# Eight gate projections in the paired stage, sample tiles of two heads in one, and a normalisation on ScalarE

## Chip, cores and metric

The kernel runs on one core of one Trainium2 chip. The metric is the device time of one execution in microseconds (us); the kernel before takes 1000.45 us in the median of 3 runs (999.62 to 1001.2). Lower is better.

## What is computed

One layer of a streaming encoder, all in float32, on 1024 prompt tokens and 64 sample tokens (T = 1088 together), with D = 1024:

```python
h = rms_norm(x, norm_w) @ w_in                     # 6144 columns
sb_q, sb_k, sb_v, sb_z, cb_q, cb_k, cb_v, cb_z, g_sb, g_cb = split(h)   # 8 heads x 64; gates 1024 columns each
# branch sb, "stick breaking": s < t only
z = q . k / 8
w[t,s] = sigmoid(z[t,s]) * prod_{s<j<t} (1 - sigmoid(z[t,j]));   o_sb = w @ v
# branch cb: softmax over a band of 8 chunks of 64 to the left, with a learned bias
p = softmax(q . k / 8 + bias[clip(q_pos - k_pos)]);   o_cb = p @ v
y = x + (sigmoid(g_sb) * ((o_sb * silu(z_sb)) @ w_proj_sb) + sigmoid(g_cb) * ((o_cb * silu(z_cb)) @ w_proj_cb)) @ w_out
```

The 64 sample tokens attend to a cache of 512 tokens and to themselves (576 keys). New keys and values are outputs too.

## The kernel before

A float32 product is made of three matmuls on a high and a low part of each operand (high x high, high x low, low x high), so every weight tile is split: ScalarE copies the high part (`W.hi`, L115), GpSimd subtracts it for the low part (`W.lo`, L122). Engines run their instructions in the order of the program; all DMAs are issued by SP in program order, besides some of the output.

The stages, in order of the program:

1. Natural projections (L464): q and k of cb and both v, tokens on the rows.
2. The paired stage (L615 to L655). A list `pairs` names blocks of 256 columns of `w_in`, two tiles of 128. Each is computed transposed by seven products instead of eight (Winograd's form of Strassen's scheme, halves of the columns, of D and of the tokens); a product is 2 chunks of 256 and 288 tokens x 12 matmuls (L634). There are 8 pairs: k and q of sb, and the gates z of both branches (kind "silu"). `emit` (L565) also knows a kind "sig", which nothing uses yet: sigmoid on ScalarE, then a store to DRAM (L575).
3. Fill. A list `units` of 16 tiles of 128 columns: eight of g_sb, stored as sigmoid, eight of g_cb, stored plain. `run_fill` (L766) is a generator that issues one matmul a step: a unit is 3 chunks of 384, 384 and 320 tokens x 8 x 3 = 72 matmuls (L773), each chunk evacuated by ScalarE (`ev_act`, L748) and stored. Weights of a later unit are loaded and split on the way (L780 to L785). Behind the units the same generator goes on with the projection of sb's output (`proj_sb`, L855, matmuls of L873). Two units run alone before the attention (L1154 to L1159).
4. The attention (L1169 to L1202). `seq` lists steps: branch, then pair of heads p (4), then tile t (the sample tile t = 8 first, then eight tiles of 128 prompt rows), then head hd. Step i does `qk(i)`, some fill, a weighted sum `av` if one is due, `tr(i-3)`, `mid(i)`, and the rest of its fill.
   - `qk`: scores by two matmuls a half (high and low part of q, L1024, L1025). In sb two sigmoids on ScalarE (L1027, L1028). In cb VectorE adds the bias and takes the row minimum of the negated scores (L1030, one custom instruction a half), and ScalarE takes the exponential with its sum (L1034).
   - `mid`: in sb a scan and a multiply on VectorE (L1044, L1045). In cb a reciprocal (L1047) and a multiply by it (L1048), both VectorE.
   - `tr`: transposes by TensorE (L1076), copied out by ScalarE (L1085, L1081) or VectorE (L1087), in turns set by the counter `flip`.
   - `av`: matmuls with v (L1115), a multiply by z on VectorE (L1118), a store.
   
   `rows(t)` is 64 for the sample tile, so it uses 64 of 128 rows, once per head. The amount of fill of a step is planned: `n_sb` and `n_cb` matmuls in all for each branch (L1161, L1162), shared out in proportion to the number of keys of the step (plus 150 in cb). When cb begins, 12 more are added at each step with t = 8 of its first pair of heads (L1185). The last unit is held back until sb's last output has been stored (L982, L1191).
   Buffers: 3 PSUM tiles for scores (a tile of over 512 keys takes two), 4 for `be`, 3 for `kp`, 4 for the transposed weights.
   `prefetch` (L1123) issues the loads of the next q, k, v and biases at fixed steps. At the start of cb, the biases of its first two heads are loaded (L1177) into memory that sb's tiles give up.
5. The rest of `proj_sb`, the projection of cb (L917), the output product (L1409) and the stores.

Of the kernel before, what the change touches and what calls it, by code (L numbers as in the profile page):

```python
# [17 lines left out]
KT = 8  # L18
# [14 lines left out]
def hybrid_step_kernel(ctx: ExitStack, tc: tile.TileContext, x_prompt, x_sample, c_sbk, c_sbv, c_cbk, c_cbv,  # L33
# [114 lines left out]
    for p in (0, 2):  # L148
        pairs += [("silu", 1536 + 128 * p, d_z["sb"][p:p + 2]), ("silu", 3584 + 128 * p, d_z["cb"][p:p + 2])]
    units = [("ev_act", 4096 + 128 * j, (AF.Sigmoid, d_g["sb"][j])) for j in range(KT)]  # L150
    units += [("ev_act", 5120 + 128 * j, (AF.Copy, d_g["cb"][j])) for j in range(KT)]

# [522 lines left out]
    G.memset(imp[:, 0:896], 0.0)  # L675
    V.tensor_copy(imp[:, 896:1024], ident)

    deferred = []
# [19 lines left out]
    def place_q(dst, src, o0, o1):  # L698

        for hd in range(2):  # L700
            for dup in range(2):
                rdma(dst[dup * 64:dup * 64 + 64, 2 * hd:2 * hd + 2, :o1 - o0], src[hd * 64:hd * 64 + 64, :, o0:o1])

    SQ, KS, VP, BI, st, wT, zts = {}, {}, {}, {}, {}, {}, {}

    def alloc_q(key, ci):
        if ci == 3:
            SQ[key, 3] = am.tile([128, 4, 64], F32R, name="sqs", bufs=1)
# [269 lines left out]
    def fill(n):  # L978
        n += owed[0]
        owed[0] = 0  # L980
        while n > 0:
# [9 lines left out]
    seq = [(b, p, t, hd) for b in ("sb", "cb") for p in range(NPAIR) for t in [8] + list(range(8))  # L991
           for hd in range(2)]

# [8 lines left out]
    def qk(i):  # L1002
        b, p, t, hd = seq[i]
        key = (b, p)
        r = rows(t)
        k0, n = band(b, t)
# [6 lines left out]
        if b == "sb":  # L1013
            kp = ax.tile([128, NP + 2], F32, name="kp", bufs=3)
            G.memset(kp[:r, n:n + 1], 0.0)
        else:
            kp = am.tile([128, 4], F32, name="sm", bufs=6)
            bt = BI[2 * p + hd]
            off = 0 if t == 8 else 640 - n
        for j, (x, y) in enumerate(hs):  # L1020
            z = psZ.tile([128, 512], F32, name="z")
            o = k0 * 128
            m = y - x
            TE.matmul(z[:r, :m], s[:, 2 * hd, q0:q0 + r], ks[:, hd, o + x:o + y], start=True, stop=False)  # L1024
            TE.matmul(z[:r, :m], s[:, 2 * hd + 1, q0:q0 + r], ks[:, hd, o + x:o + y], start=False, stop=True)  # L1025
            if b == "sb":
# [10 lines left out]
    def mid(i):  # L1037
        b, p, t, hd = seq[i]
        r = rows(t)
        k0, n = band(b, t)  # L1040
        be, kp = st[i]
        if b == "sb":
            im = imp[0:64, 960 - n:960] if t == 8 else imp[:, NP - n:NP]
            V.tensor_tensor_scan(kp[:r, n - 1::-1], kp[:r, n - 1::-1], im[:, ::-1], 0.0, op0=OP.mult, op1=OP.add)  # L1044
            V.tensor_tensor(out=be[:r, :n], in0=be[:r, :n], in1=kp[:r, 1:n + 1], op=OP.mult)  # L1045
        else:
            V.reciprocal(kp[:r, 3:4], kp[:r, 2:3])  # L1047
            V.tensor_scalar(be[:r, :n], be[:r, :n], kp[:r, 3:4], None, op0=OP.mult)  # L1048

# [5 lines left out]
    def tr(i):  # L1055
        b, p, t, hd = seq[i]
        r = rows(t)
        k0, n = band(b, t)
# [37 lines left out]
    def av(b, p, j):  # L1096
# [13 lines left out]
        for si, (kb, c0, c1) in enumerate(steps):  # L1110
# [3 lines left out]
            for hd in range(2):  # L1114
                TE.matmul(o[hd * 64:hd * 64 + 64, c0:c1], vv[:kr, kb, hd * 64:hd * 64 + 64],  # L1115
                          wT[b, p, j, hd, s // 4][:kr, s % 4, c0:c1], start=si == 0, stop=si == len(steps) - 1)
        os = zts.pop((b, p, j))
# [28 lines left out]
    def load_bias(h):  # L1146
# [4 lines left out]
        G.memset(bt[64:128, 0:64], BIG)  # L1151
        BI[h] = bt

    load_k("sb", 0, 1)  # L1154
# [5 lines left out]
    FP = 180  # L1160
    n_sb = 72 * 7  # L1161
    n_cb = 72 * (len(units) - 9) + FP  # L1162
    wt = {"sb": lambda n: n, "cb": lambda n: n + 150}
# [5 lines left out]
    for i in range(len(seq) + LAG + 1):  # L1169
# [25 lines left out]
        if 0 <= i - LAG < len(seq):  # L1195
            tr(i - LAG)
            b, p, t, hd = seq[i - LAG]
            if hd == 1 and (t % 2 == 1 or t == 8):
                avq.append((b, p, t // 2 if t < 8 else 4))
# [295 lines left out]
```

## Time and profile before

The profiled execution of the kernel before:

| | |
|---|---|
| median of 3 runs | 1000.45 us |
| span of the profiled execution | 1000.1 us |
| instructions | 20177 |
| granted TensorE clock, mean | 0.998 |
| TensorE matmul busy | 977.8 us |
| VectorE busy | 657.0 us |
| ScalarE busy | 472.9 us |
| GpSimd busy | 324.9 us |
| moved by DMA | 169.83 MB |

Rows of the profile name engines: PE is TensorE (PEld its weight loads), DVE VectorE, ACT ScalarE, POOL GpSimd, SP SyncE, which issues the DMAs (SPq its queue). A group's row gives line, engine, operation, the tile written <- the tiles read, shapes and count, then busy us and mean ns of one, then the idle time of the engine just before these instructions and what ended it. A row of the timeline begins with its start and its length in us. L12 is line 12 of the kernel before; behind the change, lines are moved by 4 to 18.

Matmuls are pipelined, so a busy PE is not PE at its peak, and the times of two neighbours overlap.

### The profile page before, as it was taken

The page shows a single profiled execution, that of the slowest core. Times are in us where ns is not written, and L with a number is a line of the kernel's source. Part 1 is how long each engine was busy: PE and PEld are TensorE (multiplying, and loading weights), DVE is VectorE, ACT ScalarE, POOL GpSimd, SP SyncE. Part 2 cuts the span into 40 slices and gives each one's busy share as a digit, 9 for nine tenths or more (in the row PEclk, how much of TensorE's full clock was granted, in tenths as well). Part 3 has the DMA queues.
Part 4 walks back from the last instruction along what each step waited for, and adds up shares of the span by engine and source line. Part 5 has one row for each costly group of instructions (what it writes and reads, how often), then busy time and mean ns, then how long its engine had stood idle before and what let it go on. Part 6 is the DMA issues. An engine that isn't in the chain of part 4 may idle for free.

```text
span 1000.1 us, 20177 instructions
## 1 busy us (share of the span) xinstructions
PE 977.8 (98%) x7512; PEld 930.8 (93%) x7512; DVE 657.0 (66%) x1233; ACT 472.9 (47%) x1075; POOL 324.9 (32%) x338
## 2 busy tenths in 40 slices
PE   5999999999999999999999999999999899999998
PEld 5999999999999999988898888898989798999998
DVE  5456674895455454099898878565766766499735
ACT  5534443444344433277676656454445434365320
POOL 3276663215445543211111101110202200386552
PEclk9999999999999999999999999999999999999999
DMA  7726577424656332786566544765656854773642
GB/s 237 224 92 221 189 249 256 150 91 150 198 155 192 102 97 85 188 228 187 146 166 159 160 114 117 206 200 152 193 150 186 253 168 147 242 224 101 196 136 89
DMA packets 180865, 169.83 MB, mean 170 GB/s; under 512 B 34912, under 2 KB 167136, under 8 KB 180640
## 3 DMA queue, kind: packets, MB, share of 16 engines
q1 hardware_dynamic: 172048, 160.23, 54.2%
q10 hardware_dynamic: 8720, 8.33, 2.6%
q8 instruction: 59, 0.97, 0.4%
q14 instruction: 38, 0.31, 0.1%
HBM read 109.78 MB, written 58.72 MB: 168 GB/s over the span
## 4 chain that ended last, share of the span: by engine, by line
PE 92%; DMA 2%; DVE 2%; ACT 1%; SPq 1%; issue 1%; POOL 1%; DVEq 0%; ACTq 0%
PE acc L464 19%; PE acc L773 18%; PE b L634 17%; PE b L1409 8%; PE o L1115 7%; PE pt L1076 6%; PE b L917 5%; PE z L1025 3%; PE z L1024 3%; PE acc L873 3%; PE pk L349 1%; DMA wrawx<-in_w_in_dram 1%; DMA gt<-d_gsb 1%; DVE be L1045 1%; PE pt L277 1%
## 5 line engine op out<-in xcount | busy, mean ns | idle before, releaser
L122 POOL TENSOR_TENSOR wlo<-wraw,whi 128x1024 fp32r<-128x1024 f32 x30 | 74.2, 2473 | 243.9 <-ACT whi L115 209.2
L773 PE MATMUL acc<-xm,whi 128*128 128x384 f32 (+1 forms) x384 | 128.5, 335 | 0.0
L1044 DVE TENSOR_TENSOR_SCAN kp<-kp,imp 64x576 f32<-64x576 f32 (+8 forms) x72 | 102.8, 1427 | 21.3 <-ACT kp L1027 21.1
L1034 ACT ACTIVATE be<-be,sm 128x640 f32<-128x640 f32 (+5 forms) x72 | 50.8, 705 | 97.1 <-DVE sm L1030 97.1
L1076 PE MATMUL pt<-ident,be 128*128 128x128 f32 (+2 forms) x608 | 90.1, 272 | 6.4 <-DVE wT L1087 3.4
L1085 ACT ACTIVATE wT<-pt 128x512 f32<-128x512 f32 (+3 forms) x130 | 63.6, 502 | 55.1 <-PE pt L1076 55.1
L1076 PEld LDWEIGHTS pt<-ident,be 128*128 128x128 f32 (+2 forms) x608 | 68.5, 140 | 18.4 <-issue 6.4
L464 PE MATMUL acc<-whi,xa 128*128 128x256 f32 x256 | 74.2, 292 | 0.0
L773 PEld LDWEIGHTS acc<-xm,whi 128*128 128x128 f32 x384 | 72.5, 189 | 1.1
L464 PE MATMUL acc<-wlox,xm 128*128 128x256 f32 x256 | 70.8, 278 | 0.0
L464 PE MATMUL acc<-whi,xm 128*128 128x256 f32 x256 | 70.8, 278 | 0.0
L464 PE MATMUL acc<-wlo,xa 128*128 128x256 f32 x256 | 70.7, 278 | 0.0
L464 PE MATMUL acc<-whix,xb 128*128 128x256 f32 x256 | 70.7, 278 | 0.0
L464 PE MATMUL acc<-whix,xm 128*128 128x256 f32 x256 | 70.6, 278 | 0.0
L1115 PE MATMUL o<-wT,vp 128*64 128x256 f32 (+1 forms) x608 | 66.7, 359 | 0.0
L1045 DVE TENSOR_TENSOR be<-be,kp 64x576 f32<-64x576 f32 (+8 forms) x72 | 60.3, 837 | 9.6
L1027 ACT ACTIVATE kp<-z 128x384 f32<-128x384 f32 (+6 forms) x112 | 54.3, 485 | 24.4 <-PE z L1025 22.9
L773 PE MATMUL acc<-xa,wlo 128*128 128x384 f32 (+1 forms) x192 | 65.4, 341 | 0.0
L773 PE MATMUL acc<-xa,whi 128*128 128x384 f32 (+1 forms) x192 | 65.3, 340 | 0.0
L773 PE MATMUL acc<-xm,wlo 128*128 128x384 f32 (+1 forms) x192 | 65.1, 339 | 0.0
L1115 PEld LDWEIGHTS o<-wT,vp 128*64 128x64 f32 x608 | 42.5, 137 | 23.7 <-issue 7.6
L773 PE MATMUL acc<-xb,whi 128*128 128x384 f32 (+1 forms) x192 | 64.0, 333 | 0.0
(298 smaller groups left out, 3017.2 us busy)
## 6 DMA issues: line engine op xcount, KB each, us to landing
wraw<-in_w_in_dram SPq DMA_DIRECT2D x35, 512.0 KB, 4.7
wrawx<-in_w_in_dram SPq DMA_DIRECT2D x13, 512.0 KB, 4.4
sq<-d_qsbT SPq DMA_DIRECT2D x32, 192.0 KB, 4.7
sq<-d_qcbT SPq DMA_DIRECT2D x32, 192.0 KB, 3.7
gt<-d_gsb SPq DMA_DIRECT2D x30, 192.0 KB, 2.7
xt<-in_x_prompt_dram SPq DMA_DIRECT2D x8, 512.0 KB, 5.1
d_kcbT<-hl SPq DMA_DIRECT2D x8, 512.0 KB, 4.5
d_qcbT<-hl SPq DMA_DIRECT2D x8, 512.0 KB, 5.6
```

Of the source, the lines that this page charges most:

```text
L122: (eng or G).tensor_tensor(out=l, in0=raw, in1=h[:].bitcast(F32), op=OP.subtract)
L464: TE.matmul(ps, x, w, start=m == 0, stop=m == len(steps) - 1)
L634: TE.matmul(ps[:, :m], w[:, hl_, k], right[s](x)[:, k, a:b], start=s < 3 and k == 0 and e == 0, stop=k == 3 and e == 2, skip_group_check=s ...
L773: TE.matmul(ps[:, :b - a], w[:, k], xk(x, k)[:, a:b], start=k == 0 and n == 0, stop=k == KT - 1 and n == 2)
L1027: A.activation(kp[:r, x:y], z[:r, :m], AF.Sigmoid, scale=-0.125)
L1034: A.activation(be[:r, :n], be[:r, :n], AF.Exp, bias=kp[:r, j:j + 1], scale=-1.0, accum_out=kp[:r, 2:3])
L1044: V.tensor_tensor_scan(kp[:r, n - 1::-1], kp[:r, n - 1::-1], im[:, ::-1], 0.0, op0=OP.mult, op1=OP.add)
L1045: V.tensor_tensor(out=be[:r, :n], in0=be[:r, :n], in1=kp[:r, 1:n + 1], op=OP.mult)
L1076: TE.transpose(pt[:kr, x, :r], be[:r, kb * 128:kb * 128 + kr], ident[:r, :r])
L1085: A.activation(w[:, sl:sl + m, q0:q0 + r], pt[:, :m, :r], AF.Copy)
L1115: TE.matmul(o[hd * 64:hd * 64 + 64, c0:c1], vv[:kr, kb, hd * 64:hd * 64 + 64], wT[b, p, j, hd, s // 4][:kr, s % 4, c0:c1], start=si == 0, ...
L1409: TE.matmul(ps[:, t], left[s](xs_, k)[:, ts_], wt_[:, k], start=s < 3 and t == k == e == 0, stop=k == 3 and e == 2, skip_group_check=s > 2 ...
```

## The change

1. The eight g_sb tiles leave `units` and become four pairs of kind "sig", at the end of `pairs`. `units` keeps the eight g_cb tiles. `n_sb` goes from 504 to 336 matmuls, `n_cb` from 684 to 276.
2. The sample tile is done once per pair of heads: rows 0 to 63 are head 0, rows 64 to 127 head 1. The tile of q (`sqs`) has 128 columns, zero where a column belongs to the other head, so that four accumulating matmuls a half give both heads' scores. The scan gets its own addend `ims`, and the sample's bias a tile of its own (`bsm`), loaded by two DMAs per pair of heads. `av` reads its halves of the one transposed tile.
3. In cb, the multiply by the reciprocal goes from VectorE to ScalarE.

```diff
+    pairs += [("sig", 4096 + 128 * j, d_g["sb"][j:j + 2]) for j in range(0, KT, 2)]
-    units = [("ev_act", 4096 + 128 * j, (AF.Sigmoid, d_g["sb"][j])) for j in range(KT)]
-    units += [("ev_act", 5120 + 128 * j, (AF.Copy, d_g["cb"][j])) for j in range(KT)]
+    units = [("ev_act", 5120 + 128 * j, (AF.Copy, d_g["cb"][j])) for j in range(KT)]
...
+    ims = ax.tile([128, 576], F32, name="ims", bufs=1)
+    G.memset(ims[:, 0:512], 0.0)
+    for h in (slice(0, 64), slice(64, 128)):
+        V.tensor_copy(ims[h, 512:576], ident[h, h])
...
+            c = 64 * hd if o0 == NP else 0
             for dup in range(2):
-                rdma(dst[dup * 64:dup * 64 + 64, 2 * hd:2 * hd + 2, :o1 - o0], src[hd * 64:hd * 64 + 64, :, o0:o1])
+                rdma(dst[dup * 64:dup * 64 + 64, 2 * hd:2 * hd + 2, c:c + o1 - o0],
+                     src[hd * 64:hd * 64 + 64, :, o0:o1])
...
+    sqs = am.tile([128, 4, 128], F32R, name="sqs", bufs=1)
+    G.memset(sqs[:].bitcast(F32), 0.0)
...
-           for hd in range(2)]
+           for hd in range(2) if t < 8 or hd == 0]
...
-            bt = BI[2 * p + hd]
+            bt = BI[2 * p + hd] if t < 8 else BI["s", p]
...
-            TE.matmul(z[:r, :m], s[:, 2 * hd, q0:q0 + r], ks[:, hd, o + x:o + y], start=True, stop=False)
-            TE.matmul(z[:r, :m], s[:, 2 * hd + 1, q0:q0 + r], ks[:, hd, o + x:o + y], start=False, stop=True)
+            parts = [(2 * h + e, h) for h in ((0, 1) if t == 8 else (hd,)) for e in range(2)]
+            for e, h in parts:
+                TE.matmul(z[:, :m], s[:, e, q0:q0 + 128], ks[:, h, o + x:o + y], start=e == parts[0][0],
+                          stop=e == parts[-1][0])
...
-            im = imp[0:64, 960 - n:960] if t == 8 else imp[:, NP - n:NP]
+            im = ims[:] if t == 8 else imp[:, NP - n:NP]
...
-            V.tensor_scalar(be[:r, :n], be[:r, :n], kp[:r, 3:4], None, op0=OP.mult)
+            A.activation(be[:r, :n], be[:r, :n], AF.Copy, scale=kp[:r, 3:4])
...
-                          wT[b, p, j, hd, s // 4][:kr, s % 4, c0:c1], start=si == 0, stop=si == len(steps) - 1)
+                          wT[b, p, j, hd, s // 4][:kr, s % 4, c0:c1] if j < 4 else
+                          wT[b, p, j, 0, s // 4][:kr, s % 4, 64 * hd:64 * hd + 64],
+                          start=si == 0, stop=si == len(steps) - 1)
...
+        if h % 2:
+            bs = BI["s", h // 2] = late["y"].tile([128, 576], F32, name="bsm", bufs=2)
+            for w in range(2):
+                src = d_rb[h - 1 + w][0:1, 127:128]
+                SP.dma_start(bs[64 * w:64 * w + 64], bass.AP(tensor=src.tensor, offset=src.offset,
+                                                             ap=[[767, 64], [1, 576]]))
...
-    n_sb = 72 * 7
-    n_cb = 72 * (len(units) - 9) + FP
+    n_sb = 72 * 5 - 24
+    n_cb = 72 * (len(units) - 2) - n_sb + FP
...
-            if hd == 1 and (t % 2 == 1 or t == 8):
+            if t == 8 or hd == 1 and t % 2 == 1:
```

More of the change, by code (lines that the diff above doesn't have):

```diff
@@ L700, in place_q @@
         for hd in range(2):
+            c = 64 * hd if o0 == NP else 0
             for dup in range(2):
-                rdma(dst[dup * 64:dup * 64 + 64, 2 * hd:2 * hd + 2, :o1 - o0], src[hd * 64:hd * 64 + 64, :, o0:o1])
+                rdma(dst[dup * 64:dup * 64 + 64, 2 * hd:2 * hd + 2, c:c + o1 - o0],
+                     src[hd * 64:hd * 64 + 64, :, o0:o1])
     SQ, KS, VP, BI, st, wT, zts = {}, {}, {}, {}, {}, {}, {}
+    sqs = am.tile([128, 4, 128], F32R, name="sqs", bufs=1)
+    G.memset(sqs[:].bitcast(F32), 0.0)
     def alloc_q(key, ci):
         if ci == 3:
-            SQ[key, 3] = am.tile([128, 4, 64], F32R, name="sqs", bufs=1)
+            SQ[key, 3] = sqs
         else:
@@ L1004, in qk @@
         key = (b, p)
-        r = rows(t)
+        r = 128
         k0, n = band(b, t)
@@ L1038, in mid @@
         b, p, t, hd = seq[i]
-        r = rows(t)
+        r = 128
         k0, n = band(b, t)
@@ L1056, in tr @@
         b, p, t, hd = seq[i]
-        r = rows(t)
+        r = 128
         k0, n = band(b, t)
```

## Prediction

> **What bounds the kernel now.** I read the profile in this order: busy time by engine and the chain that ended last, to find the engine that sets the end; the table of stretches, cut where that chain changes from one matmul line to the next; then, in the two attention stretches, the groups by line of the engines beside PE; at last single instructions in order of time.
>
> ```profile
> PE 977.8 (98%) x7512; PEld 930.8 (93%) x7512; DVE 657.0 (66%) x1233; ACT 472.9 (47%) x1075; POOL 324.9 (32%) x338
> PE 92%; DMA 2%; DVE 2%; ACT 1%; SPq 1%; issue 1%; POOL 1%; DVEq 0%; ACTq 0%
> ```
>
> PE is busy 98% of the span and holds 92% of the chain, so what counts is PE work, as long as PE stays the last one in each stage. Whether it does is read from the stretches (columns: length, then busy time and count of PE, PEld, DVE, ACT, POOL, the granted clock, DMA share, GB/s):
>
> ```profile
> core 0: us, PE busy (x) PEld busy (x) DVE busy (x) ACT busy (x) POOL busy (x), PEclk, DMA share, GB/s
> 0.00:226.65 226.65, 216.46 (x1842) 214.93 (x1843) 146.93 (x273) 100.33 (x230) 101.06 (x122) 1.00 0.57 190
> 226.65:399.06 172.41, 172.41 (x1385) 171.55 (x1385) 89.14 (x174) 68.41 (x159) 82.67 (x56) 1.00 0.46 140
> 399.06:422.80 23.74, 23.74 (x147) 23.73 (x146) 2.16 (x5) 5.16 (x9) 5.72 (x6) 1.00 0.65 174
> 422.80:621.07 198.27, 194.77 (x1401) 173.00 (x1400) 171.83 (x186) 136.19 (x334) 24.39 (x76) 0.99 0.63 164
> 621.07:846.20 225.13, 221.26 (x1603) 200.29 (x1600) 146.39 (x465) 104.74 (x251) 32.83 (x32) 1.00 0.65 184
> 846.20:1000.10 153.90, 149.14 (x1142) 147.31 (x1142) 100.51 (x132) 58.08 (x93) 78.24 (x47) 1.00 0.52 161
> ```
>
> The rows are: natural projections; paired stage (8 pairs); two units of fill; first branch (sb); second branch (cb); merge and output. In sb, DVE is busy 171.8 of 198.3 us: it is the runner-up by little. In cb it has 146.4 of 225.1. The fill in both branches is what keeps PE ahead of them, and the change takes most of it away.
>
> **The change, part by part.** The terms are made against this execution: span 1000.1 us, 0.35 below the median of 1000.45.
>
> *Eight units become four pairs.* The chain gives two stretches without a gap:
>
> ```profile
> 300.67 98.39 PE b L634 x792
> 399.06 23.73 PE acc L773 x144
> ```
>
> A matmul of the paired stage takes 98.39/792 = 0.1242 us, so a pair (7 products x 2 chunks x 12 = 168) takes 20.9 us and four take **+83.5**. A fill matmul takes 23.73/144 = 0.1648, so eight units of 72 cost 94.9 where they were. Beside the paired stretch DVE, ACT and POOL are half busy (172.4 us against 89.1, 68.4, 82.7); a gate pair needs less of DVE than a silu pair (no multiply), and its weight loads and gate stores replace those of two units on SP. I take nothing more for it; loads landing late are in the range.
>
> *Where the fill goes missing.* The planner's amounts fall from 504 to 336 matmuls in sb and from 684 to 276 in cb. The extra 12 at the start of cb is added once, no longer for two tiles: 708 become 288. So sb loses 168, cb 420, and 12 end up in the tail: **+2.0**.
>
> *sb.* PE work falls by 168 x 0.1648 = 27.7. Stacking leaves the score matmuls equal in number (2 halves x 4 instead of 2 heads x 2 x 2) and halves the transposes. Five of a 64-row tile and five of a full one:
>
> ```profile
> 640.02 0.44 PE pt L1076 x5
> 682.70 0.55 PE pt L1076 x5
> ```
>
> Four pairs x (0.88 - 0.55) = 1.3 less. PE: 194.8 - 27.7 - 1.3 = 165.8 us. DVE by line in this stretch, POOL's weight split over both branches, and single scans in order of time:
>
> ```profile
> L1044 DVE TENSOR_TENSOR_SCAN kp<-kp,imp 64x576 f32<-64x576 f32 (+8 forms) x72 | 102.8, 1427 | 21.3 <-ACT kp L1027 21.1
> L1045 DVE TENSOR_TENSOR be<-be,kp 64x576 f32<-64x576 f32 (+8 forms) x71 | 59.0, 831 | 9.5
> L1118 DVE TENSOR_TENSOR zt<-o,zt 128x256 f32<-128x256 f32 (+1 forms) x19 | 7.2, 378 | 11.9 <-PE o L1115 10.3 <-DMA sq<-d_qsbT 1.6
> ```
> ```profile
> L122 POOL TENSOR_TENSOR wlo<-wraw,whi 128x1024 fp32r<-128x1024 f32 x17 | 42.5, 2502 | 186.3 <-ACT whi L115 158.4 <-DMA vs<-d_cbv 14.1 <-PE pt L1076 8.6
> ```
> ```profile
> 510.78 2.28 DVE L1044 TENSOR_TENSOR_SCAN kp<-kp,imp 128x1024 f32<-128x1024 f32 x1
> 516.31 3.59 DVE L1044 TENSOR_TENSOR_SCAN kp<-kp,imp 128x1024 f32<-128x1024 f32 x1
> 521.65 1.34 DVE L1044 TENSOR_TENSOR_SCAN kp<-kp,imp 64x576 f32<-64x576 f32 x1
> 523.80 1.35 DVE L1044 TENSOR_TENSOR_SCAN kp<-kp,imp 64x576 f32<-64x576 f32 x1
> ```
>
> The multiply pauses 0.13 us behind its scan (9.5 in all), so DVE's own chain is 171.8 + 9.5 = 181.3 of 198.3. A sample tile takes 523.80 - 521.65 = 2.15; duration goes with columns, so one of 128 rows I take the same: four go, -8.6. The same scan takes 2.28 us, and 3.59 where POOL's weight split runs: +1.3 each; the splits in sb go with the fill from 7 (504/72) to 4.7 (336/72), -3.0. DVE: 169.7 us, now **above** PE's 165.8. Today the stage ends 3.5 above its bound; with two engines this close I add 4.3 and get 174: **-24.3**, of which PE's own saving would have been 29.
>
> [...]
>
> *cb.* PE: 221.3 - 420 x 0.1648 (69.2) - 1.3 = 150.8. Beside it runs a ring through DVE and ACT: DVE adds the bias and takes the row minimum, ACT does the exponential and its sum, DVE the reciprocal and, until now, the normalising, and only then the next tile's bias.
>
> ```profile
> 820.70 0.48 DVE L1030 CUSTOM_DVE_ANT_0 be<-z,bias 128x320 f32<-128x320 f32 x1
> 821.34 0.55 DVE L1030 CUSTOM_DVE_ANT_0 be<-z,bias,sm 128x320 f32<-128x320 f32 x1
> 821.99 0.83 ACT L1034 ACTIVATE be<-be,sm 128x640 f32<-128x640 f32 x1 [2.45 <-DVE sm L1030]
> 822.73 0.19 ACT L1034 ACTIVATION_READ_ACCUMULATOR be<-be,sm 128x1 f32 x1
> 822.82 0.58 ACT L1085 ACTIVATE wT<-pt 128x512 f32<-128x512 f32 x1
> 823.14 0.55 DVE L1048 TENSOR_SCALAR be<-be,sm 128x640 f32<-128x640 f32 x1
> ```
> ```profile
> 809.45 0.55 DVE L1030 CUSTOM_DVE_ANT_0 be<-z,bias 128x384 f32<-128x384 f32 x1
> 810.99 0.42 DVE L1048 TENSOR_SCALAR be<-be,sm 128x384 f32<-128x384 f32 x1
> ```
>
> To the point where the normalising starts, a tile of 640 takes 823.14 - 820.70 = 2.44, one of 384 takes 1.54. With it on ACT the ring is that short: per pair 8 x 2.44 + 8 x 1.54 (the smaller tiles at the 384 one) + about 2.2 for one sample tile = 34, four pairs 136, below PE's 151. ACT pays 72 - 4 = 68 instructions more. No row shows ACT's plain scaling of this tile; the bounds are DVE's mean for it, 603 ns, and ACT's own exponential over the same tile, 705 ns in the mean and 830 at 640 columns (groups of the cb stretch):
>
> ```profile
> L1048 DVE TENSOR_SCALAR be<-be,sm 128x640 f32<-128x640 f32 (+5 forms) x72 | 43.4, 603 | 2.5
> L1034 ACT ACTIVATE be<-be,sm 128x640 f32<-128x640 f32 (+5 forms) x72 | 50.8, 705 | 97.1 <-DVE sm L1030 97.1
> L1034 ACT ACTIVATE be<-be,sm 128x640 f32<-128x640 f32 x32 | 26.6, 830 | 50.7 <-DVE sm L1030 50.7
> L115 ACT ACTIVATE whi<-wraw 128x1024 fp32r<-128x1024 f32 x10 | 10.5, 1049 | 0.0
> L1030 DVE CUSTOM_DVE_ANT_0 be<-z,bias 128x320 f32<-128x320 f32 (+5 forms) x72 | 34.6, 480 | 10.0 <-PE z L1025 6.1 <-DMA bias<-d_rb 3.2
> L748 ACT ACTIVATE sg<-acc 128x384 f32<-128x384 f32 (+1 forms) x22 | 10.0, 456 | 0.4 <-PE acc L773 0.3
> ```
>
> I take 0.70, the exponential being the nearest row (same engine, same tile): 48 us. ACT then has 104.7 + 48 - 4 (four exponentials and their sums) - 11 (22 gate copies become some 6, ten weight splits six) = 138 in a stage of 151 to 160: inside, with a tenth to spare. The first cb tile waits for a bias load today (3.2); now two more loads are issued ahead of it and I take 1 to 2 more. So cb = 150.8 + 3.9 (what it loses today) + 3.3 for the later start and the closer race = 158: **-67.1**.
>
> Sum: 83.5 + 2.0 - 24.3 - 67.1 = -5.9: span 994.2, time **994.5 us**.
>
> **The rivals.**
> *PE stays the bound everywhere.* Today's losses of 3.5 and 3.9 stay as they are: sb 169.3, cb 154.7, sum 83.5 + 2.0 - 29.0 - 70.4 = -13.9: 986.5. For it: DVE and PE within 4 us in sb, three tiles of lag between them. Against: the DVE sum is the higher one.
>
> *ACT's queue sets cb (slower).* On ACT the normalising of a tile stands ahead of the next exponential, and ahead of it a copy of transposed blocks that waits for PE. If ACT's instructions run in single file, a 640 tile costs 0.83 + 0.19 + 0.58 + 0.83 = 2.43, plus 0.2 for the reciprocal and 0.27 of waiting for PE: 2.9; a small one 1.9 by the same rows at 384. 32 x 2.9 + 32 x 1.9 + 4 x 2.6 + 9 for six splits and six gate copies = 173: 15 above the forecast, 1009.5. It turns the sign once cb takes over 164, 0.1 us per tile above my forecast. For it: no slack in ACT beyond a tenth. Against: the normalising is only needed three tiles later, and DVE's next bias (1.2) runs beside it.
>
> [...]
>
> *sb does not follow PE down.* If DVE goes on waiting for PE's products (11.9 us at L1118) as today, sb falls only by DVE's 8.6 + 3.0: 186.7, which is 12.7 over the forecast: 1007. Against: these waits come of PE being late, and PE is what gets lighter.
>
> That the pairs don't replace the units is out: the instruction order shows 672 more paired and 576 fewer fill matmuls.
>
> **How the numbers follow.** The forecast (989 to 998) gets 0.42, PE-bound 0.18, both faster: 0.60. That the closer race eats just the gain 0.12. ACT's queue 0.18 and sb's DVE 0.10: slower 0.28. About 0.2% (2 us) is what a measurement of this kernel can tell from no change. The range 984 to 1010 reaches from below the PE-bound case to the ACT one at its price; about 2 in 10 is left for what goes beyond them. The unknown costs, a 128-row sample tile (2.15 to 2.6) and ACT's scaling (0.60 to 0.83), move 2 and 6 us at most within it.
>
> **What would show it.** Twelve gapless pairs and a paired stretch near 256 us show the first term; sb (first score to first cb score) near 174 with DVE busy near 92% (86.7% now) the second; cb near 158 with PE still above 93% the third. ACT waiting little and PE waiting on ACT at the transposes in cb would show the slower rival. Wrong from the start I would be if the paired matmul cost more than 0.1242 with 12 pairs in a row, 0.01 being 6.7 us.

## The result, and the profile after

The changed kernel takes **1032.65 us** (median of 4 runs, 1029.85 to 1033.99) where the kernel before took 1000.83 on the same chip: ratio 1.0322, 95% interval 1.0307 to 1.0336. It is slower by 3.2%; forecast were 994.5 us and a range from 984 to 1010. The profiled execution took 1032.53 us, its span is 1030.75, against 1000.13 before.

The first two rows are busy time by engine and the chain that ended last, of the kernel after. Then come its stretches (columns as in the prediction, lines of the kernel after from here on), and the last two of the kernel before, cut once more at the start of cb's last `av`, a mark that both kernels have.

```profile
PE 981.3 (95%) x7568; PEld 925.4 (90%) x7568; DVE 636.9 (62%) x1188; ACT 514.3 (50%) x1142; POOL 345.9 (34%) x356
PE 78%; DVE 9%; ACT 4%; DMA 4%; issue 2%; SPq 1%; POOL 0%; DVEq 0%; ACTq 0%
```
```profile
0.00:226.20 226.20, 216.09 (x1842) 214.47 (x1843) 146.87 (x273) 100.43 (x230) 101.15 (x122) 1.00 0.57 190
226.20:481.82 255.62, 255.62 (x2058) 254.76 (x2057) 119.34 (x232) 99.64 (x228) 121.04 (x84) 1.00 0.43 129
481.82:505.39 23.57, 23.57 (x145) 23.57 (x144) 1.91 (x4) 4.75 (x8) 6.84 (x8) 1.00 0.70 195
505.39:692.65 187.26, 172.50 (x1216) 146.86 (x1214) 160.53 (x175) 124.57 (x302) 20.37 (x70) 0.97 0.60 157
692.65:869.24 176.59, 161.46 (x1171) 136.04 (x1171) 105.29 (x372) 127.48 (x285) 17.92 (x26) 0.97 0.72 201
869.24:1030.80 161.56, 152.04 (x1146) 149.72 (x1145) 102.91 (x133) 57.44 (x91) 78.53 (x47) 0.99 0.51 158
```
```profile
621.07:848.04 226.97, 222.72 (x1614) 201.35 (x1611) 146.81 (x466) 105.50 (x253) 32.83 (x32) 1.00 0.64 183
848.04:1000.10 152.06, 147.68 (x1133) 146.25 (x1132) 100.08 (x131) 57.32 (x91) 78.24 (x47) 1.00 0.52 162
```

PE is still busy 95%, but its share of the chain fell from 92% to 78%, and DVE (9%), ACT (4%) and DMA (4%) have most of the rest: the chain now passes from one engine to another. By stage:

| | change measured | forecast | miss |
|---|---|---|---|
| paired stage | +83.2 | +83.5 | -0.3 |
| sb | -11.0 | -24.3 | +13.3 |
| cb, to its last `av` | -50.4 | -67.1 | +16.7 |
| the rest | +9.5 | +2.0 | +7.5 |
| natural projections, two units | -0.6 | 0 | -0.6 |
| sum | +30.7 | -5.9 | +36.6 |

The price was paid as forecast, the gain came in part. Three views of the kernel after show where. The first is one place in sb in order of time (start and length in us; in brackets the idle time before, and what ended it):

```profile
595.92 2.46 POOL L122 TENSOR_TENSOR wlo<-wraw,whi 128x1024 fp32r<-128x1024 f32 x1 [7.53 <-ACT whi L115]
596.07 3.52 DVE L1054 TENSOR_TENSOR_SCAN kp<-kp,ims 128x576 f32<-128x576 f32 x1
600.40 0.68 DVE L1097 COPY wT<-pt 128x512 f32<-128x512 f32 x1
601.14 1.12 PE L1086 MATMUL pt<-ident,be 128*128 128x128 f32 x4 [2.76 <-DVE wT L1097]
603.25 5.42 PE L1125 MATMUL o<-wT,vp 128*64 128x256 f32 x32
608.72 0.42 DVE L1130 TENSOR_TENSOR zt<-o,zt 128x256 f32<-128x256 f32 x1 [6.12 <-PE o L1125]
```

Read it downwards. GpSimd splits a weight; the scan beside it takes 3.52 us instead of 1.35, so the copy behind it in DVE's queue comes late; PE waits 2.76 us for that copy; then PE's sums run slowly, and DVE waits 6.12 us for them. Why PE is slow there, the second view says. It cuts out three stretches of 3.41 us in which PE pauses, and what follows each; the column after POOL is the granted clock:

```profile
596.99:600.40 3.41, 1.39 (x12) 1.11 (x10) 3.28 (x2) 1.70 (x5) 1.46 (x3) 1.00 0.53 155
600.40:607.23 6.83, 6.09 (x28) 4.06 (x30) 1.94 (x6) 1.25 (x3) 0.30 (x3) 0.50 0.00 0
648.19:651.60 3.41, 0.28 (x3) 0.14 (x1) 3.28 (x5) 1.01 (x3) 0.20 (x2) 1.00 0.33 93
651.60:655.01 3.41, 3.35 (x14) 2.93 (x16) 1.26 (x5) 1.79 (x4) 0.20 (x2) 0.51 0.00 0
696.01:699.43 3.42, 1.32 (x10) 1.10 (x8) 1.11 (x1) 0.00 (x0) 0.00 (x0) 1.00 0.33 91
699.43:709.66 10.23, 4.44 (x21) 4.42 (x22) 2.37 (x11) 4.98 (x12) 0.58 (x4) 0.50 0.88 240
```

Behind these three stretches, in which PE was busy 1.39, 0.28 and 1.32 of 3.41 us, the clock is granted at half for 6.83, 3.41 and 10.23 us. With a fourth such place at 894 (PE busy 1.48 of 3.41, then 3.41 at half) that is 23.9 us at half. A fill matmul at half (653.28) took 0.67 us, one of the same shape at full clock (735.74) 0.34. PE was busy 17.3 of the 23.9, so at most half of that, 8.6 us, is lost, an estimate from these figures; before, there was one stretch of 3.4 at half. At 600.40 the clock fell when PE had paused 2.02 us (of 2.76 in all).

The third view is the start of cb:

```profile
695.90 1.23 DVE L1055 TENSOR_TENSOR be<-be,kp 128x1024 f32<-128x1024 f32 x1
697.15 0.81 SPq L1161 DMA_DIRECT2D bias<-d_rb  x2
698.01 1.11 SPq L1169 DMA_DIRECT2D bsm<-d_rb  x2
702.65 0.46 DVE L1040 CUSTOM_DVE_ANT_0 be<-z,bsm 128x288 f32<-128x288 f32 x1 [5.52 <-DMA bsm<-d_rb]
703.82 0.77 ACT L1044 ACTIVATE be<-be,sm 128x576 f32<-128x576 f32 x1 [9.18 <-DVE sm L1040]
704.59 0.57 ACT L1095 ACTIVATE wT<-pt 128x512 f32<-128x512 f32 x1
705.22 1.97 PE L1086 MATMUL pt<-ident,be 128*128 128x128 f32 x8 [7.89 <-ACT wT L1095]
```

The loads wait for sb's last multiply (697.13), whose memory they take; `bsm` goes out behind the two biases; DVE waits 5.5 us for it, ACT's exponential 9.2 for DVE, and behind that exponential stands the copy for which PE waits 7.9. The clock falls in the middle of this wait (699.43) and is still at half when PE goes on.

### The profile page after: what moved, and what is told of

It is laid out like the page before. It is cut to its first block, busy times and chain, and to the rows that moved or that the text cites. A ratio compares the mean times of both kernels' runs of the same rounds, so it can differ in the third digit from the quotient of the medians.

```text
span 1030.8 us, 20364 instructions
## 1 busy us (share of the span) xinstructions
PE 981.3 (95%) x7568; PEld 925.4 (90%) x7568; DVE 636.9 (62%) x1188; ACT 514.3 (50%) x1142; POOL 345.9 (34%) x356
## 4 chain that ended last, share of the span: by engine, by line
PE 78%; DVE 9%; ACT 4%; DMA 4%; issue 2%; SPq 1%; POOL 0%; DVEq 0%; ACTq 0%
PE b L634 24%; PE acc L464 19%; PE b L1427 7%; PE o L1125 6%; PE acc L781 5%; PE b L925 5%; PE pt L1086 4%; DVE kp L1054 4%; PE z L1034 3%; PE acc L881 2%; DVE be L1055 2%; ACT be L1044 2%; DVE be L1040 1%; DVE wT L1097 1%; ACT wT L1095 1%
## 5 line engine op out<-in xcount | busy, mean ns | idle before, releaser
L1086 PE MATMUL pt<-ident,be 128*128 128x128 f32 (+1 forms) x568 | 92.8, 287 | 24.1 <-DVE wT L1097 12.7
L1086 PEld LDWEIGHTS pt<-ident,be 128*128 128x128 f32 (+1 forms) x568 | 67.8, 144 | 38.8 <-DVE wT L1097 16.2
L1054 DVE TENSOR_TENSOR_SCAN kp<-kp,imp 128x128 f32<-128x128 f32 (+7 forms) x64 | 90.4, 1412 | 0.3 <-ACT kp L1037 0.3
L1034 PE MATMUL z<-ks,sq 128*128 128x320 f32 (+5 forms) x384 | 85.1, 328 | 0.4
L1034 PEld LDWEIGHTS z<-ks,sq 128*128 128x128 f32 x384 | 66.8, 190 | 2.7 <-DVE sm L1040 1.7
L781 PE MATMUL acc<-xm,whi 128*128 128x384 f32 (+1 forms) x192 | 65.8, 343 | 0.0
L1055 DVE TENSOR_TENSOR be<-be,kp 128x128 f32<-128x128 f32 (+8 forms) x68 | 55.4, 815 | 9.1
L1037 ACT ACTIVATE kp<-z 128x384 f32<-128x384 f32 (+6 forms) x104 | 51.7, 497 | 15.6 <-PE z L1034 12.0
L1044 ACT ACTIVATE be<-be,sm 128x640 f32<-128x640 f32 (+5 forms) x68 | 47.4, 697 | 24.2 <-DVE sm L1040 23.4
L642 DVE TENSOR_TENSOR u<-b,s 128x256 f32<-128x256 f32 (+1 forms) x48 | 20.7, 439 | 56.2 <-PE b L634 54.9
L1038 ACT ACTIVATE be<-z 128x384 f32<-128x384 f32 (+6 forms) x104 | 52.1, 501 | 0.0
L1058 ACT ACTIVATE be<-be,sm 128x640 f32<-128x640 f32 (+5 forms) x68 | 47.4, 697 | 9.0 <-DVE sm L1057 8.6
```

The costliest lines, as they stand in the source:

```text
L781: TE.matmul(ps[:, :b - a], w[:, k], xk(x, k)[:, a:b], start=k == 0 and n == 0, stop=k == KT - 1 and n == 2)
L1034: TE.matmul(z[:, :m], s[:, e, q0:q0 + 128], ks[:, h, o + x:o + y], start=e == parts[0][0], stop=e == parts[-1][0])
L1044: A.activation(be[:r, :n], be[:r, :n], AF.Exp, bias=kp[:r, j:j + 1], scale=-1.0, accum_out=kp[:r, 2:3])
L1086: TE.transpose(pt[:kr, x, :r], be[:r, kb * 128:kb * 128 + kr], ident[:r, :r])
```

## The experiments

The medians of the changed kernels are of 4 to 10 runs, and each ratio is to runs of the kernel before on the same chip. "sb", "cb", "rest" are the stretches of the table above in one profiled execution, which can lie some 5 us off its median. The last column is the time at half clock, without the kernel's last 5 us. Theories carry letters; each is told in the first expectation that names it.

| kernel | us | ratio to before, 95% | sb | cb | rest | at half clock |
|---|---|---|---|---|---|---|
| before | 1000.45 | | 198.4 | 227.0 | 152.1 | 3.4 |
| after | 1032.65 | 1.0307 to 1.0336 | 187.3 | 176.6 | 161.5 | 23.9 |
| e1 scaling on VectorE | 1048.24 | 1.0453 to 1.0500 | 185.8 | 193.6 | 161.5 | 17.1 |
| e2 pairs only | 1049.45 | 1.0469 to 1.0507 | 185.8 | 201.5 | 153.1 | 10.2 |
| e3 no pairs | 950.00 | 0.9475 to 0.9511 | 184.4 | 176.9 | 159.8 | 10.2 |
| e4 units back | 1002.51 | 1.0012 to 1.0030 | 192.6 | 224.9 | 162.2 | 10.2 |
| e5 `bsm` first | 1031.53 | 1.0269 to 1.0328 | 185.5 | 174.0 | 160.4 | 13.7 |
| e6 `bsm` early | 1025.41 | 1.0223 to 1.0275 | 185.6 | 170.7 | 160.2 | 10.2 |
| e7 two pairs | 1018.15 | 1.0155 to 1.0195 | 188.7 | 200.4 | 160.6 | 17.1 |
| e8 lag of 4 | 1029.90 | 1.0271 to 1.0309 | 179.7 | 178.9 | 161.0 | 17.1 |
| e9 `av` multiply late | 1036.13 | 1.0346 to 1.0377 | 189.3 | 178.7 | 160.2 | 27.3 |
| e10 `mid` late | 1026.58 | 1.0252 to 1.0283 | 184.3 | 173.1 | 160.7 | 13.7 |
| e11 fill at large tiles | 1030.65 | 1.0289 to 1.0320 | 187.0 | 176.6 | 159.9 | 20.5 |
| e12 four edits | 1019.73 | 1.0177 to 1.0211 | 187.1 | 165.0 | 160.3 | 10.2 |
| e13 half multiply | 1012.16 | 1.0092 to 1.0129 | 168.2 | 173.3 | 160.3 | 6.8 |
| e14 no low part | 1019.50 | 1.0172 to 1.0224 | 176.2 | 174.8 | 160.6 | 17.1 |
| e15 three orders | 1025.43 | 1.0233 to 1.0272 | 180.5 | 178.3 | 159.3 | 13.7 |
| e16 units, three orders | 999.83 | 0.9976 to 0.9997 | 190.8 | 222.5 | 161.6 | 3.4 |
| e17 before, no low part | 996.34 | 0.9949 to 0.9974 | 194.3 | 226.7 | 151.7 | 0 |
| e18 three causes away | 1009.31 | 1.0059 to 1.0109 | 176.2 | 162.9 | 161.5 | 3.4 |

### The parts of the change

Theory A: with thin fill the branches are no longer bound by TensorE but by the coupling of the queues. Rival B: the scaling blocks ScalarE's queue. Rival C: the longer paired stage lowers the clock.

e1, the changed kernel with the scaling back on VectorE:

```diff
-            A.activation(be[:r, :n], be[:r, :n], AF.Copy, scale=kp[:r, 3:4])
+            V.tensor_scalar(be[:r, :n], be[:r, :n], kp[:r, 3:4], None, op0=OP.mult)
```


> The changed kernel with one part undone: the normalisation of the second branch is back on VectorE. Theory A (with most of the fill gone, neither branch is bound by TensorE any more; the rings through VectorE and ScalarE and their coupling to TensorE set the length): taking the normalisation off VectorE was a help, so undoing it makes the second branch longer, by about 0.55 us for each of the 32 tiles of 640 keys and 0.4 for the others, some 30 us in all: 1050 to 1065. Theory B (the normalisation blocks ScalarE's queue, which sets the second branch): undoing it makes the kernel faster, 1010 to 1025. Theory C (a lower clock behind the long paired stage makes the difference): no large change, 1030 to 1040.

Measured 1048.24, just under A's range: the scaling on ScalarE is worth 15.6 us here. B, by which this would be faster, falls.

e2, the kernel before with part 1 of the change alone:

```diff
+    pairs += [("sig", 4096 + 128 * j, d_g["sb"][j:j + 2]) for j in range(0, KT, 2)]
-    units = [("ev_act", 4096 + 128 * j, (AF.Sigmoid, d_g["sb"][j])) for j in range(KT)]
...
+    n_sb = 72 * 5 - 24
+    n_cb = 72 * (len(units) - 2) - n_sb + FP
```


> The kernel before with the first part of the change alone: eight gate tiles as four pairs, the reduced amounts of fill, sample tiles and normalisation as before. Theory A: both branches then hang on VectorE's larger sums (first branch 181 us with pauses, second branch on the long ring of about 3.3 us per 640 tile), so it is clearly slower than the full change: 1050 to 1075. Theory B: without the normalisation on ScalarE it is faster than the full change, 1010 to 1030. Theory C: about the same as the full change, 1030 to 1040, with a mean clock near 0.988.

Measured 1049.45, 1.2 from e1: in sum, stacking is worth next to nothing. By stage it is not: with it (e1) cb is 7.9 us shorter, and the rest of the kernel 8.4 longer.

e3, the changed kernel without the pairs, so that g_sb is not computed (its loads read g_cb):

```diff
-    pairs += [("sig", 4096 + 128 * j, d_g["sb"][j:j + 2]) for j in range(0, KT, 2)]
```


> The changed kernel without the four gate pairs; the first gate is left out and the unsquashed second gate is read in its place, so the first branch is merged with wrong gates. What is left is the cost of everything else. Theory A: exactly the pairs' 83 us less, 947 to 952, of which 1000.8 - 950 = 50 us is all that taking eight units (95 us of TensorE) out of the branches gives. Theory C: without the 82 us of dense matmuls the clock stays near 0.998 and the branches shrink as well: 935 to 942. Theory B says nothing on it.

Measured 950.00: the pairs cost 82.7 us, and the branches are nearly as long as with them (sb 184.4, cb 176.9). C falls.

e4, the changed kernel with the edit of e2 undone (sixteen units, the old amounts, no gate pair):


> The changed kernel with its first part undone: all sixteen units are fill again, with the amounts of before; sample tiles stay stacked and the normalisation stays on ScalarE. Theory A: TensorE is the bound again, and these two parts save the half of the sample transposes and some waits: 990 to 999. Theory B: ScalarE's queue sets the second branch also here only if its sum is over TensorE's; with the fill back it is not, 998 to 1004. Theory C: clock as before, 0.998.

Measured 1002.51, outside A's range. So, in sum, stacking and scaling give nothing where fill is full: sb and cb are 5.8 and 2.1 us shorter than in the kernel before, and the rest is 10.1 longer. And taking eight units out (94.9 us of TensorE) gives 1002.5 - 950.0 = 52.5, less than the pairs cost. That is the result in one line; the rest asks where 42 us stayed.

e7, half of it (two pairs, twelve units):

```diff
-    pairs += [("sig", 4096 + 128 * j, d_g["sb"][j:j + 2]) for j in range(0, KT, 2)]
+    pairs += [("sig", 4096 + 128 * j, d_g["sb"][j:j + 2]) for j in (0, 2)]
+    units = [("ev_act", 4096 + 128 * j, (AF.Sigmoid, d_g["sb"][j])) for j in range(4, KT)]
...
-    n_sb = 72 * 5 - 24
+    n_sb = 420
```


> The changed kernel with two of the four gate pairs: four g_sb tiles stay units, 420 and 480 matmuls of fill in the two branches. With no pair moved it takes 1002.5 us, with four 1032.65; the pairs cost 20.7 us each, and removing eight units gave 52.5 us of the 95 us of TensorE time that they hold. If every unit removed gives the same (6.6 us), it is 1017 to 1018 us. Theory A (TensorE sets the branches as long as there is enough fill, and the pauses grow as it thins): the first four units give more than the last four: 1002 to 1012. If already the first units give nothing: above 1020.

Measured 1018.15. Less 41.4 for two pairs that is 976.8, half-way between 1002.5 and 950.0: every unit gives 6.6 us of its 11.9, the first as the last. That A has a threshold, below which all is gained, is refuted for the time as a whole. The two branches differ, though (one execution each, e4 against the changed kernel): sb gives back 5.3 us for 168 fill matmuls, which are 27.7 us of TensorE, and cb 48.3 for 408, which are 67.2. In sb the first half of them gave 3.9 (e7) and the second 1.4.

### The start and the order of cb

e5, `bsm` loaded ahead of the two biases at the start of cb (the expectation says at each place; for the later pairs of heads the edit leaves it behind them); e6, `bsm` in memory not shared with sb, and its first load in sb's last pair. The diff of each in turn (`load_bsm` holds what `load_bias` did for `bsm`):

```diff
+                load_bsm(0)
                 load_bias(0)
                 load_bias(1)
```
```diff
-            bs = BI["s", h // 2] = late["y"].tile([128, 576], F32, name="bsm", bufs=2)
+        bs = BI["s", p] = am.tile([128, 576], F32, name="bsm", bufs=2)
...
+        if b == "sb" and p == NPAIR - 1 and t == 4:
+            load_bsm(0)
```


> The changed kernel with one order reversed: at each place that loads biases, the sample's tile bsm is loaded ahead of the two biases instead of behind them. Theory D (the start of the second branch is a load of its own: TensorE stands 8.1 us there behind the first sample step, which waits for bsm, and then runs 10.2 us at half clock, some 13 us of the loss of 37): two transfers of 0.15 MB no longer stand behind two of 0.33 MB, so the stall shrinks by 2 to 4 us and with it perhaps the half clock: 1022 to 1030 us. Theory A (the loss is the coupling of queues and rings in every tile, and a wait at one place is only where it shows): 1030 to 1034.

> The changed kernel with the sample tile bsm in memory that is not shared with the first branch, its first load issued five tiles before that branch ends and not behind its last multiply. The first step of the second branch then waits for no load; the biases are first needed one step later. Theory D: the 8.1 us stall at 697 and the half clock behind it go: 1017 to 1025 us. Theory A: the first step gains, the next waits instead: 1028 to 1034.

e5 gave 1031.53 (the order of these loads hardly counts), e6 1025.41, just over D's range: that `bsm` is late costs 7.2. PE's waits in both branches, after and then e6 (total, times, longest):

```profile
PE pt L1086 <- DVE wT L1097: 12.7, 10, 3.2
PE pt L1086 <- ACT wT L1095: 10.4, 8, 7.9
```
```profile
PE pt L1086 <- ACT wT L1095: 4.7, 8, 2.3
```

The wait of 7.9 us is gone, the 12.7 for DVE stay as they were.

e10, in cb `mid(i-1)` in step i, so that VectorE doesn't stand at the reciprocal for the exponential of the same step:

```diff
-        if i < len(seq):
-            mid(i)
+        for x in range(max(0, i - 1), min(i + 1, len(seq))):
+            if (seq[x][0] == "sb") == (x == i):
+                mid(x)
```


> The changed kernel with the second branch's mid one step later: reciprocal and scaling of tile i-1 are issued in step i. In the changed kernel VectorE waits 25.6 us in the second branch at the reciprocal for ScalarE's exponential of the same step, and ScalarE 23.4 us at the exponential for VectorE. Theory A, sharpened: this ring within a step is what holds the second branch over TensorE's own time; without it 1016 to 1026 us. If it is slack, or the shorter distance to the transposes costs as much: 1029 to 1036.

DVE's waits in cb, after and then e10:

```profile
DVE sm L1057 <- ACT be L1044: 25.6, 37, 2.3
DVE zt L1130 <- PE o L1125: 19.4, 17, 2.8
```
```profile
DVE zt L1130 <- PE o L1125: 22.9, 17, 2.8
DVE sm L1057 <- ACT be L1044: 0.3, 1, 0.3
```

1026.58: 25.6 us of waiting became 0.3, and the time fell by 6.1, between the two expectations, since part of it turns up at other waits.

e8, four tiles of distance:

```diff
-        be = am.tile([128, NP], F32, name="be", bufs=4)
+        be = am.tile([128, NP], F32, name="be", bufs=5)
...
-    LAG = 3
+    LAG = 4
```


> The changed kernel with one more tile of distance: transposes four tiles behind the scores instead of three, five buffers of be instead of four; nothing else changes. Theory A (the chain scores, ScalarE, VectorE, transposes of one tile is too long for three tiles' distance once the fill between them is thin): 1012 to 1025 us. Rival E (the pauses come from the two tiles pt and three tiles z of PSUM and from load order, not from the distance): 1029 to 1036.

1029.90, in E's range: 2.8 less; sb gains 7.6 and cb loses 2.3. e9, the multiply of `av`'s result (L1130; `scales` holds it) behind `mid` in VectorE's queue:

```diff
         if i < len(seq):
             mid(i)
+        while scales:
+            scales.pop(0)()
```


> The changed kernel with one instruction later in VectorE's queue: the multiply of av's result by z stands behind the step's mid instead of ahead of it. In the changed kernel VectorE waits 15.5 us in the first branch and 19.4 us in the second at this multiply for TensorE's sums, with the next scans or biases queued behind it. Theory A, sharpened (the queues wait for each other inside a step, and VectorE's order lets TensorE's lateness through): 1018 to 1027 us. If those waits only fill time that VectorE would lose anyway: 1030 to 1034.

1036.13: slower by 3.5, which neither side expected. So that VectorE stands at L1130 (35 us in both branches) ahead of its other work is not what costs the time; the waits show a PE that is late already. e11, sb's fill away from the small tiles:

```diff
-    wt = {"sb": lambda n: n, "cb": lambda n: n + 150}
+    wt = {"sb": lambda n: 0 if n in (128, 256, 576) else n, "cb": lambda n: n + 150}
```


> The changed kernel with the first branch's 336 matmuls of fill laid elsewhere: none at the steps of 576, 128 and 256 keys, all at those of 384 to 1024 keys in proportion to the keys. Theory F (in the large tiles VectorE's scan and multiply are longer than TensorE's work of the step, and in the small ones TensorE, with the sums and transposes of the large ones, is late; fill stands where TensorE is late already): TensorE's waits shrink, 1020 to 1028 us. If the waits come from the distances alone: 1030 to 1036.

1030.65: theory F falls. e12, the edits of e6, e9, e10 and e11 together:


> The changed kernel with four edits together: bsm loaded early, the multiply of av late, mid of the second branch one step later, and the first branch's fill at the large tiles. Theory A: what TensorE loses in the branches (52 us over its own times there against 14 before) mostly goes: 1000 to 1012 us, under 1000 if all of it goes. Rival (each removes a wait that another replaces): above 1017.

1019.73. cb comes to 165.0, sb stays at 187.1: whatever held sb was none of these.

### What holds sb

e13 leaves out half of VectorE's multiply in sb, and with it half of each row's scaling:

```diff
-            V.tensor_tensor(out=be[:r, :n], in0=be[:r, :n], in1=kp[:r, 1:n + 1], op=OP.mult)
+            V.tensor_tensor(out=be[:r, :n // 2], in0=be[:r, :n // 2], in1=kp[:r, 1:n // 2 + 1], op=OP.mult)
```


> The changed kernel with half of the first branch's multiply left out (only the first half of each row is multiplied by the scan): some 27 us less of VectorE's 160.5 us in that branch, nothing less for TensorE. Theory G (VectorE's queue sets the first branch, with no room to catch up): the branch comes down from 187 us to TensorE's own 163 to 172, the whole to 1010 to 1018 us. Rival (pauses of TensorE by distances and the clock, VectorE has slack): 1027 to 1034.

e14 leaves out GpSimd's low part of the unit weights in the attention:

```diff
-                            W.split(("u", j + 1) if j + 1 < len(units) else ("p", 0))
+                            if j + 1 < len(units):
+                                W.hi(("u", j + 1))
+                                W.raw.pop(("u", j + 1))
+                                W.sp["u", j + 1] = (W.sp["u", j + 1][0],) * 2
+                            else:
+                                W.split(("p", 0))
```


> The changed kernel without GpSimd's low part of the fill's weights in the attention (the high part stands for it, so the product is short of a term; TensorE's work is the same). Theory G: scans beside a split take 1.1 to 2.2 us longer, and with VectorE as the bound of the first branch the five splits there cost 5 to 10 us: 1022 to 1028 us. Rival (VectorE has slack): 1030 to 1034.

Stretch sb of e13, then of e14:

```profile
505.42:673.63 168.21, 164.47 (x1216) 144.05 (x1214) 143.91 (x177) 123.42 (x302) 18.60 (x70) 1.00 0.67 176
```
```profile
505.55:681.80 176.25, 169.12 (x1215) 145.25 (x1214) 152.43 (x177) 123.80 (x302) 6.39 (x65) 0.99 0.64 168
```

Nothing was taken from PE in either. With 16.6 us less of DVE's busy time (27 were expected) sb is 19.1 shorter, and PE is busy 98% of it again: VectorE sets sb. And five splits (9 GpSimd splits in both branches, 4 left) cost 11.0 us there, 13.1 in all. Groups of sample scans, after and then e14 (line 1059 there), say how:

```profile
L1054 DVE TENSOR_TENSOR_SCAN kp<-kp,ims 128x576 f32<-128x576 f32 x4 | 7.6, 1895 | 20.6 <-ACT kp L1037 20.6
```
```profile
L1059 DVE TENSOR_TENSOR_SCAN kp<-kp,ims 128x576 f32<-128x576 f32 x4 | 5.4, 1352 | 20.6 <-ACT kp L1042 20.6
```

One of the four scans met a split and lost 2.2 us, nearly the whole 2.46 of it; two scans of other tiles lost 1.9 and 2.2 (562.53 and 638.54 in the changed kernel). In sum, DVE's busy time falls by 8.1 us, 1.6 a split.

e17, the same taken out of the kernel before:


> The kernel before without GpSimd's low part of the fill's weights in the attention (the high part stands for it, TensorE's work is the same). In the changed kernel this gave 13.1 us. Theory G (what delays VectorE costs time only where TensorE has no fill to spare; before, TensorE sets the branches): 995 to 1000 us. Rival (the split costs the same in both): 986 to 990.

996.34: 13 splits fewer (17 to 4) give 4.0 us, 0.3 a split, against 2.6 in the changed kernel. Seven of the 13 are in sb. There VectorE's busy time falls by 10.3 us (171.8 to 161.5), about as much per split as in the changed kernel, and the stage by 4.2, which is 0.6 a split against 2.2. Full fill hid most of it.

### What can be put together

e15, the orders of e6, e8 and e10:


> The changed kernel with bsm loaded early, the second branch's mid one step later and four tiles of distance (five be). By themselves these gave 7.2, 6.1 and 2.8 us. If they are three different waits: 1014 to 1018 us, and less if the half clock goes with them; if they share one: 1022 to 1027.

1025.43, no better than e6 alone: what e8 gained in sb it lost in cb. e16, the same with sixteen units and no pairs:


> The same three edits with all sixteen units back in the branches (no gate pair, amounts as in the kernel before), so stacked sample tiles and ScalarE's scaling with a better order. Without the three edits this took 1002.5 us. Theory A (with full fill TensorE is the bound and hides such waits; its pauses there are some 14 us in both branches): 996 to 1001 us. If the orders are worth as much as with thin fill: 986 to 991.

999.83, which is 0.1% under before, the interval just clear of 1: too little to call a gain. sb and cb together are 12.1 us shorter than before, and the rest is 9.5 longer. e18, the changed kernel without the three causes (e6, e10, e14):


> The changed kernel without GpSimd's low part in the attention, with bsm loaded early and the second branch's mid one step later (alone 13.1, 7.2 and 6.1 us). If they are three separate causes: 1004 to 1010 us. If they share a wait: 1012 to 1018. Below 1000 only if TensorE's half clock goes with them.

1009.31: 23.3 less, of 26.4 if they were quite separate. Its stretches:

```profile
505.84:682.06 176.22, 169.07 (x1216) 145.29 (x1215) 152.43 (x177) 123.80 (x302) 6.38 (x65) 0.99 0.64 168
682.06:844.97 162.91, 155.06 (x1171) 133.41 (x1170) 101.93 (x370) 123.70 (x285) 17.92 (x26) 1.00 0.77 216
844.97:1006.40 161.43, 151.42 (x1146) 148.91 (x1145) 103.01 (x133) 57.36 (x91) 77.28 (x47) 1.00 0.51 158
```

sb and cb now lie 2 and 3 us over the forecast (174, and 227.0 - 67.1 = 159.9 by this cut), with 3.4 us at half clock in this execution instead of 23.9. But e14 and e18 also take 8.1 us from VectorE in sb, which the forecast had counted, so they are no account of the miss by themselves. No version that computes the whole result was found that beats the kernel before by more than 0.2%, which is what its measurement can tell.

## Why the prediction was wrong

**The pairs: right.** Forecast +83.5, measured +83.2 in the stage and 82.7 in the time (e3).

**The work of each engine: right for VectorE and for the scaling, too low for TensorE.** In sb DVE's chain was put at 169.7 us, PE at 165.8. After has these groups of DVE in sb (the last number of the second is the pause behind the scan):

```profile
L1054 DVE TENSOR_TENSOR_SCAN kp<-kp,imp 128x128 f32<-128x128 f32 (+7 forms) x63 | 88.1, 1398 | 0.3 <-ACT kp L1037 0.3
L1055 DVE TENSOR_TENSOR be<-be,kp 128x128 f32<-128x128 f32 (+8 forms) x67 | 54.2, 809 | 8.9
L1130 DVE TENSOR_TENSOR zt<-o,zt 128x256 f32<-128x256 f32 (+1 forms) x18 | 6.7, 374 | 15.5 <-PE o L1125 15.5
```

160.5 busy and 8.9 of pauses are 169.4. PE was busy 172.5 in sb, and 161.5 in cb, where 150.8 were forecast (152.2 by this cut). Half clock makes up to 4.7 and 2.2 of that; the other 2 and 7 stay open, though with fewer pauses of PE they shrink (155.1 in cb in e18). ScalarE's scaling, taken at 0.70 us, is 0.697 here:

```profile
L1058 ACT ACTIVATE be<-be,sm 128x640 f32<-128x640 f32 (+5 forms) x68 | 47.4, 697 | 9.0 <-DVE sm L1057 8.6
```

**sb: the step that failed is "with two engines this close I add 4.3".** The stage lies 17.9 us over DVE's chain (187.3 - 169.4), and DVE is busy 86% of it, not 92%. Nearly all of the 17.9 is VectorE waiting in its turn: 15.5 at L1130 for PE's sums (the row above; the three long waits are 2.8, 6.1 and 5.2), and 1.8 before the first scan. PE in turn waits for VectorE's copies, before and then after (sb alone):

```profile
PE pt L1076 <- DVE wT L1087: 3.0, 2, 2.4
```
```profile
PE pt L1086 <- DVE wT L1097: 12.0, 8, 3.2
```

So two engines with nearly equal sums were not late at the same time: a late DVE makes PE pause, behind two of these pauses the clock is at half, and then DVE waits for PE. Four tiles of distance took 7.6 off the stage (e8), so three were too few in this stage. The splits were counted only as far as they go away (-3.0); the five that stay cost 11.0 (e14), of which 8.1 is VectorE's own time, held already in the 169.7, so they make some 3 of the 13.3 us missed. The rival "sb does not follow PE down" gave 186.7 for this stage and had a chance of 0.10. It was right in the number, and DVE did go on waiting at that line (15.5 us, 11.9 before). What spoke against it, that PE gets lighter and so less late, failed: PE's lateness came from DVE's copies.

**cb: the steps that failed are "I take 1 to 2 more" for the first load, and the 3.3 for the later start and "the closer race".** `bsm` costs 7.2 (e6), since the wait for it goes on through ACT's queue to PE and its clock. The ring of 2.44 us was left out of the sum since four pairs of it, 136, lie below PE's 151. But it holds a wait: the reciprocal stands in VectorE's queue for the exponential of its own step, 25.6 us in all, with work for PE behind it, and e10 gets 6.1 of them back. ACT's queue, the rival with 0.18, put cb 15 over the forecast, where 16.7 came: right in the number, not in the cause. With the same scaling on ACT, e18 brings cb to 162.9, and with it back on VectorE the kernel is slower (e1).

**The granted clock was no term of the sum.** It went from 3.4 to 23.9 us at half inside the kernel, at most 8.6 us of loss by the estimate above. Each of the four places goes with a pause of PE (2.76, 3.20, 7.89 and 3.46 us), and with the three causes gone it is back at 3.4 in the profiled execution. The gains of e6, e10, e14 and e18 contain their part of it.

**The rest: "12 end up in the tail, +2.0" became +9.5.** All kernels with stacked sample tiles have 159.3 to 162.2 us there, those without 151.7 to 153.1. That is 13 more fill matmuls (97 instead of 84 behind the last `av`, some 2 us), and for the most part a longer wait of PE for the projection's multiply, which waits for the gate's load. Before, and then after:

```profile
DVE xm L877 <- DMA gt<-d_gsb: 2.1, 2, 1.9
PE acc L873 <- DVE xm L877: 0.5, 1, 0.5
```
```profile
DVE xm L885 <- DMA gt<-d_gsb: 7.5, 3, 3.6
PE acc L881 <- DVE xm L885: 5.6, 4, 3.5
```

What makes these loads late has no experiment and stays open. In e3, e4 and e16 the longer rest is there without any pair, and in e1 without the scaling on ScalarE, so it belongs to the stacking. It eats what the stacking gains in the branches.

Of the 36.6 us missed, 7.5 lie in the rest. e18 takes away 23.3; but by the prediction's own rule sb without the five splits would be put at 165.8 + 4.3 = 170, not 174, so some 19 of them count. The last 9 or so are what sb (176.2) and cb (162.9) of e18 still lie over 170 and 159.9. This split is an estimate from these figures.

## What to carry to other kernels

Filler work between two engines has two values: its own time, and the waits that it covers. Price the second before you move it, and stage by stage: here a unit gave back 6.6 of its 11.9 us in the mean (an estimate by the figures behind e7: some 2.3 in sb and 8.5 in cb), while the work put in its place cost 10.3. When the sums of two engines come close (here 169.7 and 165.8 us were forecast in sb, and the stage took 187.3), don't take the larger one with a small loss; look for what interrupts the new bound (a GpSimd split, a load at a change of stage), and count that a pause of TensorE of 2.8 us was followed by 6.8 at half clock, up to 3.0 more lost by the estimate above (PE was busy 6.1 of them).

## What the runs showed of the hardware

- The clock was granted at half after a stretch of 3.41 us in which TensorE was busy 1.39 us, with a longest pause of 2.02; 9 of the 12 matmuls in it were transposes. In the kernel before, too, 1.02 us busy of 3.42, with a pause of 2.40, was followed by half clock:

```profile
572.20:575.62 3.42, 1.02 (x8) 0.89 (x7) 3.42 (x3) 1.29 (x5) 2.10 (x4) 1.00 0.68 193
575.62:579.03 3.41, 3.41 (x18) 2.70 (x18) 2.35 (x4) 1.64 (x4) 0.20 (x2) 0.51 0.00 1
```

- No threshold in busy time comes out of these runs: in e11 half clock followed 1.80 us busy of 3.41 (longest pause 1.28), in the changed kernel 1.58 of 3.42 was followed by full clock. e11, then after:

```profile
508.64:512.05 3.41, 1.80 (x27) 1.52 (x27) 2.94 (x7) 1.95 (x6) 0.30 (x3) 1.00 0.89 234
512.05:515.46 3.41, 3.41 (x15) 3.20 (x14) 3.07 (x6) 1.65 (x5) 0.20 (x2) 0.50 0.83 242
```
```profile
730.14:733.56 3.42, 1.58 (x14) 0.83 (x13) 1.12 (x5) 3.29 (x7) 0.29 (x2) 1.00 0.79 214
733.56:736.97 3.41, 3.41 (x27) 3.13 (x24) 2.67 (x4) 2.05 (x5) 2.81 (x4) 1.00 0.93 298
```

- A VectorE scan beside a GpSimd split took 3.52 us instead of 1.35: it lost 2.2 us, beside a split of 2.46. The mean over all five splits of sb was 1.6 us of VectorE's time.
- A 576-column scan over 128 rows took 1.35 us, as one over 64 rows did.
